# Two weight sums of the mLSTM values built by VectorE instead of accumulating transfers, in a Strassen-like product on one Trainium2 core

## The chip, the cores and the metric

The kernel runs on one core of a Trainium2 chip. The metric is the device time of one execution in microseconds; of several executions the median is taken. TensorE (PE) multiplies, VectorE (DVE) and ScalarE (ACT) do elementwise work, GpSimd (POOL) some more of it; transfers are issued from the queues of SyncE (SP), ScalarE and POOL.

## What is computed

One decoder block with two branches, on x of 512 x 1024 in float32: RMSNorm, one wide input projection, an mLSTM branch (4 heads of 256, chunked in the reference), a sparse attention branch (8 heads of 64), gates, two branch projections, one output projection, residual and RMSNorm. Cut to what the change touches:

```python
hN = _rmsnorm(x, norm_g[l])
p = _split_in(hN @ w_in[l])          # w_in: 1024 x 8992
mh = _mlstm(mq, mk, p["m_v"].reshape(B, T, M_HEADS, M_HEAD_DIM), ...)
```

The change lies in the values `m_v`: a product of h (512 tokens x 1024) with the 1024 x 1024 columns of `w_in` that begin at 2048.

## The kernel before

Every float32 operand of a large product is split into a high part (rounded to TensorE's float32r) and a low remainder, and a product is made of three passes: high x high, high x low, low x high. The split of a weight tile is one ScalarE copy (`wh`) and one VectorE subtraction (`wl`); `weights` (L156) loads a raw tile `wr` and splits it, `halves_of` (L1173) splits a tile that lies in SBUF. Each of `wr`, `wh` and `wl` has three buffers. h lies transposed in SBUF, split into `hTh` and `hTl`.

The order of the work comes from a stream of jobs (L176): each job has a load and a generator of matmuls, and the loads of the next two jobs are written before a job's matmuls begin. A scheduler then orders the instructions of each engine ahead of the run, by their place in the program and by what its own timing takes for ready; on the chip each engine follows its order.

The values are made by seven products of half-sized blocks in place of eight (Strassen's scheme in Winograd's form). h is cut into four quarters of 256 tokens x 512 channels, the weights into quarters W00, W01, W10, W11 of 512 x 512 (`wq[i][j]`: rows i, columns j). A product is 24 matmuls of 128x128 on 128x512 and two jobs, one for each half (`q`) of its 512 channels; `strip_product` (L1202) writes them, two blocks of 128 tokens (`l`) after one another in two PSUM banks. In their order the products use

1. h quarter 0 with W00 (into bank X; copied into Y),
2. h quarter 1 with W10 (onto X, then stored as values),
3. a sum of h (S1) with W00 + W01 (`first_sum`, bank V),
4. a sum of h (S2) with W00 + W01 + W11 (`second_sum`, onto Y),
5. a sum of h (S3) with W11 (`last_quarter`, onto V, then combined by VectorE and stored),
6. a sum of h (S4) with W01 + W11 (`third_sum`, onto Y, then combined and stored),
7. h quarter 3 with W00 + W01 + W11 + W10 (`fourth_sum`, onto Y, then stored).

The weight sums lie in `E`, two tiles of 128 x 4 x 512. They are built by transfers alone: `onto` (L1098) either loads a 512 KB half from memory through SP's queue or adds it in flight to what lies there, through POOL's queue. E[0] begins as W00 + W01, is split for the third product, and is then loaded anew as W01 + W11 for the sixth. E[1] begins as W00 + W01 + W11, is split for the fourth product, and then gets W10 added for the seventh. That makes six plain loads and ten accumulating ones. E, and the tiles for the sums of h, lie in memory that attention used before, so none of this can begin before attention's last instruction.

The sums of h (`sum_of_h`, L1118) are VectorE's: the first (two joined quarters, a difference, a split) stands ahead of the first product, the second in the first product's second job, the third in the second product's first job, a difference that the fourth needs (`a11 - a21`, number 0) in its second job, the split of the fourth in the fourth product's first job.

Around the products: two gate projections (48 matmuls) run just before, and the projections of q and k for the first head (`convs(0)`, L1287) just behind, all 128-column jobs of the stream (L214 to L218).

Of the kernel before, what the change touches and what calls it, by code (L numbers as in the profile page):

```python
# [11 lines left out]
F32 = mybir.dt.float32  # L12
# [66 lines left out]
def build(  # L79
# [1015 lines left out]
    def piece_of(src, q):  # L1095
        return src[:, 2 * q : 2 * q + 2]

    def onto(e, q, i, j, add=True):  # L1098
        if add:
            nc.gpsimd.dma_start(piece_of(E[e], q), piece_of(wq[i][j], q), accum_op=OP.add)  # L1100
        else:
            nc.sync.dma_start(piece_of(E[e], q), piece_of(wq[i][j], q))

    for q in range(2):
        onto(0, q, 0, 0, False)
        onto(0, q, 0, 1)
    for q in range(2):
        onto(1, q, 0, 0, False)
        onto(1, q, 0, 1)
        onto(1, q, 1, 1)  # L1110
    gates_ahead(2, sg0)

    a21, a22, a11, a12 = whole = [raws(i, (4, 256), f"r{i}") for i in range(4)]
# [59 lines left out]
    def halves_of(raw):  # L1173
        hi = wp.tile([128, 2, 512], F32R, name="wh", tag="wh", bufs=3)
        lo = wp.tile([128, 2, 512], F32R, name="wl", tag="wl", bufs=3)
        split(raw, hi, lo)
        return hi, lo

    def first_sum(q):
        w = halves_of(piece_of(E[0], q))  # L1180
        if q:
            E[0] = st.tile([128, 4, 512], F32, name="E", tag="E0")
            for i in range(2):
                onto(0, i, 0, 1, False)
                onto(0, i, 1, 1)
        return w

    def second_sum(q):
        w = halves_of(piece_of(E[1], q))
        onto(1, q, 1, 0)  # L1190
        return w

    def last_quarter(q):
        return from_w(1, 1)(q)

    def third_sum(q):
        return halves_of(piece_of(E[0], q))

    def fourth_sum(q):
        return halves_of(piece_of(E[1], q))  # L1200

    def strip_product(lhs, load, bank, first, post, pre=((), ())):  # L1202
        def gen(q):
            def run(w):
                for n in pre[q]:
                    sum_of_h(n)
                for l in range(2):
                    ps = bank(l)
                    for j in range(2):
                        a, b = lhs(2 * q + j, l)  # L1210
                        c, d = w[0][:, j], w[1][:, j]
                        begin = first and q + j == 0
                        pe.matmul(ps, a, c, start=begin, stop=False, skip_group_check=not first)  # L1213
                        yield
                        pe.matmul(ps, a, d, start=False, stop=False, skip_group_check=not first)  # L1215
                        yield
                        pe.matmul(ps, b, c, start=False, stop=q + j == 2, skip_group_check=not first)  # L1217
                        if l + j < 2:
                            yield
                    if q == 1:  # L1220
                        post(l)

            return run

        for q in range(2):
            stream.add(lambda q=q: load(q), gen(q))
# [10 lines left out]
    def negated(ps, t):  # L1237
        dve.scalar_tensor_tensor(t, ps, -1.0, t, OP.mult, OP.subtract)
        return t

    sum_of_h(1)
    strip_product(of_h(0), from_w(0, 0), X, True, after1, ((), (2,)))
    strip_product(of_h(1), from_w(1, 0), X, False, lambda l: store_values(l, 0, X(l)), ((3,), (0,)))
    strip_product(of_sum(1), first_sum, V, True, after5)
    strip_product(of_sum(2), second_sum, Y, False, after6, ((4,), ()))
    strip_product(
        of_sum(3), last_quarter, V, False, lambda l: store_values(l, 1, negated(V(l), kept["p12"][:, l]))
    )
    strip_product(
        of_sum(4), third_sum, Y, False, lambda l: store_values(2 + l, 1, negated(Y(l), kept["p22"][:, l]))  # L1250
    )
    strip_product(of_h(3), fourth_sum, Y, False, lambda l: store_values(2 + l, 0, Y(l)))

# [489 lines left out]
```

## Time and profile before

| | |
|---|---|
| median of three runs | 634.84 us (634.75 to 635.98) |
| the profiled execution | 636.86 us, span 634.8 us |
| granted TensorE clock, mean | 0.988 |
| PE, DVE, ACT, POOL busy | 613.4, 450.8, 326.2, 89.7 us |
| loads into E: plain (SP), accumulating (POOL) | 6 and 10, of 512 KB |

The profile is of one execution. Busy time of an engine is the time in which it had an instruction in flight; matmuls overlap, so their pace is read from start to start. An idle time is put down to the instruction or transfer that ended it. Most lines of the listing appear as L94, since a helper there issues all instructions of ScalarE, VectorE and POOL; they are told apart by their tiles. `pp`, `ps`, `pt` are the PSUM banks: in this stage `ps` is X, `pt` is V and `pp` is Y. L1213, L1215 and L1217 are the three passes of `strip_product`.

### The profile page before, as it was taken

To read this page: it belongs to the slowest core of one execution; us is meant where nothing else is said; L and a number is where in the kernel's file an instruction comes from. 1 tells how busy PE (TensorE), PEld (TensorE's weight loads), DVE (VectorE), ACT (ScalarE), POOL (GpSimd) and SP (SyncE) were. 2 spreads that over 40 slices of the span, in tenths; PEclk is the share of its full clock that TensorE was granted. 3 is DMA by queue.
4 is the path that set the end of the run, shared out by engine and by line. 5 is a ranking of instruction groups with operands and counts; after the bars stand their busy time and mean duration, and the time that the engine had idled before them with its cause. 6 is when DMAs were issued, how large, how long until landed. Compare 5 with 4: busy or idle time off the path is not lost.

```text
span 634.8 us, 8493 instructions
## 1 busy us (share of the span) xinstructions
PE 613.4 (97%) x3033; PEld 510.0 (80%) x3033; DVE 450.8 (71%) x860; ACT 326.2 (51%) x621; POOL 89.7 (14%) x169
## 2 busy tenths in 40 slices
PE   8999999999999999999499999999999999999995
PEld 6988888888788888787378888888888888888884
DVE  5876776876766956678376788787687665358885
ACT  5775556556546557444356445545445222334554
POOL 6320012212322213212300000000000100000013
PEclk9999999999999999999699999999999999999998
DMA  9546522221222122249954313223222266333313
GB/s 294 153 115 182 136 81 66 68 65 36 68 67 67 42 62 64 62 165 254 203 116 130 100 35 99 73 68 93 67 93 74 66 215 177 108 101 132 132 34 133
DMA packets 92410, 68.14 MB, mean 107 GB/s; under 512 B 3104, under 2 KB 80068, under 8 KB 92368
## 3 DMA queue, kind: packets, MB, share of 16 engines
q1 hardware_dynamic: 89070, 61.30, 33.7%
q0 software_dynamic: 2720, 5.24, 4.6%
q10 hardware_dynamic: 578, 1.05, 0.4%
q8 instruction: 24, 0.39, 0.3%
q14 instruction: 18, 0.15, 0.1%
HBM read 64.44 MB, written 2.10 MB: 105 GB/s over the span
## 4 chain that ended last, share of the span: by engine, by line
PE 47%; DMA 4%; DVE 3%; ACT 1%; POOL 1%; issue 1%; ACTq 0%; POOLq 0%; SPq 0%; DVEq 0%
PE pp L216 12%; PE pp L214 12%; PE pp L218 12%; DMA E<-w_in 4%; DVE wl L94 1%; PE ps L174 1%; DVE s L94 1%; PE pp L1215 1%; PE pp L1213 1%; PE ps L173 1%; PE ps L172 1%; PE pp L1217 1%; PE pt L1360 1%; PE pt L1362 1%; PE pt L1361 1%
## 5 line engine op out<-in xcount | busy, mean ns | idle before, releaser
L214 PE MATMUL pp<-hTh,wh 128*128 128x512 f32 (+1 forms) x488 | 191.5, 392 | 0.0
L216 PE MATMUL pp<-hTl,wh 128*128 128x512 f32 (+1 forms) x488 | 190.9, 391 | 0.0
L218 PE MATMUL pp<-hTh,wl 128*128 128x512 f32 (+1 forms) x488 | 190.6, 391 | 0.0
L94 DVE TENSOR_TENSOR wl<-wr,wh 128x1024 fp32r<-128x1024 f32 x84 | 103.4, 1233 | 38.0 <-ACT wh L94 36.7
L94 ACT ACTIVATE wh<-wr 128x1024 fp32r<-128x1024 f32 x84 | 88.8, 1058 | 72.3 <-PE pp L216 47.4
L218 PEld LDWEIGHTS pp<-hTh,wl 128*128 128x128 f32 x488 | 91.9, 188 | 16.4
L214 PEld LDWEIGHTS pp<-hTh,wh 128*128 128x128 f32 x488 | 91.9, 188 | 16.1
L216 PEld LDWEIGHTS pp<-hTl,wh 128*128 128x128 f32 x488 | 92.0, 189 | 15.6
L94 POOL TENSOR_SCALAR P<-P,st,gates 128x128 f32<-128x128 f32 (+1 forms) x64 | 45.2, 720 | 186.7 <-DVE st L94 136.2
L94 ACT ACTIVATE P<-P,st 128x128 f32<-128x128 f32 (+3 forms) x64 | 35.8, 559 | 38.1 <-DVE st L94 37.6
L94 DVE CUSTOM_DVE_ANT_0 P<-ps,cst 128x128 f32<-128x128 f32 (+3 forms) x64 | 30.4, 486 | 23.0 <-PE ps L939 21.8
L94 ACT ACTIVATE pth<-pt 128x512 fp32r<-128x512 f32 (+1 forms) x64 | 26.8, 435 | 29.0 <-PE pt L955 22.3
L94 DVE TENSOR_TENSOR ptl<-pt,pth 128x512 fp32r<-128x512 f32 (+1 forms) x64 | 30.1, 483 | 14.4 <-ACT pth L94 14.2
L94 DVE SCALAR_TENSOR_TENSOR u<-pp,prm,u 128x511 f32<-128x511 f32 (+2 forms) x48 | 35.7, 744 | 0.7
L94 ACT ACTIVATE th<-u 128x512 f32<-128x512 f32 x16 | 10.1, 631 | 41.5 <-DVE u L94 41.5
L94 POOL TENSOR_TENSOR rlr<-va,mhalf 128x4 f32<-128x4 f32 x4 | 5.1, 1287 | 184.6 <-DVE va L94 184.6
L955 PE MATMUL pt<-cst,P 128*128 128x128 f32 x160 | 28.8, 277 | 1.8 <-POOL P L94 1.0
L955 PEld LDWEIGHTS pt<-cst,P 128*128 128x128 f32 x160 | 20.1, 141 | 11.6 <-DVE ptl L94 4.8
L214 PE MATMUL pp<-yah,wh 128*128 128x512 f32 x64 | 24.9, 389 | 0.0
L216 PE MATMUL pp<-yal,wh 128*128 128x512 f32 x64 | 24.9, 389 | 0.0
L218 PE MATMUL pp<-yah,wl 128*128 128x512 f32 x64 | 24.9, 389 | 0.0
L968 PE MATMUL po<-ptl,vsw 128*128 128x512 f32 (+1 forms) x64 | 21.2, 332 | 0.0
(378 smaller groups left out, 1135.1 us busy)
## 6 DMA issues: line engine op xcount, KB each, us to landing
wr<-w_in SPq DMA_DIRECT2D x66, 512.0 KB, 3.9
E<-w_in POOLq DMA_DIRECT2D x10, 512.0 KB, 8.7
wr<-w_out SPq DMA_DIRECT2D x8, 512.0 KB, 3.9
wr<-w_branch_a SPq DMA_DIRECT2D x8, 512.0 KB, 4.4
E<-w_in SPq DMA_DIRECT2D x6, 512.0 KB, 5.6
wr<-w_branch_b SPq DMA_DIRECT2D x4, 512.0 KB, 3.5
T<-w_out SPq DMA_DIRECT2D x4, 512.0 KB, 5.0
s<-x SPq DMA_DIRECT2D x8, 256.0 KB, 4.0
```

Of the source, the lines that this page charges most:

```text
L94: ins = fn(*args, **kw)
L172: pe.matmul(ps, a, c, start=start and i == 0, stop=False)
L173: pe.matmul(ps, a, d, start=False, stop=False)
L174: pe.matmul(ps, b, c, start=False, stop=stop and i == n - 1)
L214: pe.matmul(ps, a, c, start=k == 0, stop=False)
L216: pe.matmul(ps, a, d, start=False, stop=False)
L218: pe.matmul(ps, b, c, start=False, stop=k == nk - 1)
L955: pe.transpose(pt[:, (qb - kb) * 128 : (qb - kb) * 128 + 128], P[:, POFF[qb] + kb * 128 : POFF[qb] + kb * 128 + 128], ident,)
L968: pe.matmul(po[:, kb * 128 :], vl, tl[:, :n], start=False, stop=False)
L1213: pe.matmul(ps, a, c, start=begin, stop=False, skip_group_check=not first)
L1215: pe.matmul(ps, a, d, start=False, stop=False, skip_group_check=not first)
L1217: pe.matmul(ps, b, c, start=False, stop=q + j == 2, skip_group_check=not first)
```

## The change

The weight sums of the third and of the sixth product are no longer accumulated in flight. E[0] is loaded as W01 alone, and E[1] later, after the split of the third product's sum, as W01 alone. The raw tile of W00, which the first product loads anyway, is added to E[0] by VectorE right behind its split (`first_quarter`), and the raw tile of W11, which the fifth product loads, to E[1] (`last_quarter`). So E[0] is W00 + W01 for the third product. Then W11 is added to it in flight for the fourth, and W10 for the seventh: one tile serves three products in turn. E[1] becomes W01 + W11 for the sixth. There are four plain loads, four accumulating ones and four additions on VectorE.

The sums of h are moved: the first into the first product's first job, the second and third into the two jobs of the second product, a11 - a21 into the third product's first job, the fourth where it was. They come one per job.

The sixth product is written block by block: its first job only holds its weights back, and its second writes all twelve matmuls of the first block and then all twelve of the second.

```diff
     for q in range(2):
-        onto(0, q, 0, 0, False)
-        onto(0, q, 0, 1)
-    for q in range(2):
-        onto(1, q, 0, 0, False)
-        onto(1, q, 0, 1)
-        onto(1, q, 1, 1)
+        onto(0, q, 0, 1, False)
     gates_ahead(2, sg0)
...
+    def plain(i, j, q, e):
+        raw = wp.tile([128, 2, 512], F32, name="wr", tag="wr", bufs=3)
+        nc.sync.dma_start(raw, piece_of(wq[i][j], q))
+        w = halves_of(raw)
+        dve.tensor_tensor(piece_of(E[e], q), piece_of(E[e], q), raw, OP.add)
+        return w
+
+    def first_quarter(q):
+        return plain(0, 0, q, 0)
+
     def first_sum(q):
         w = halves_of(piece_of(E[0], q))
-        if q:
-            E[0] = st.tile([128, 4, 512], F32, name="E", tag="E0")
-            for i in range(2):
-                onto(0, i, 0, 1, False)
-                onto(0, i, 1, 1)
+        onto(0, q, 1, 1)
+        onto(1, q, 0, 1, False)
         return w
 
     def second_sum(q):
-        w = halves_of(piece_of(E[1], q))
-        onto(1, q, 1, 0)
+        w = halves_of(piece_of(E[0], q))
+        onto(0, q, 1, 0)
         return w
 
     def last_quarter(q):
-        return from_w(1, 1)(q)
+        return plain(1, 1, q, 1)
 
     def third_sum(q):
+        return halves_of(piece_of(E[1], q))
+
+    def fourth_sum(q):
         return halves_of(piece_of(E[0], q))
...
-    def strip_product(lhs, load, bank, first, post, pre=((), ())):
+    def strip_product(lhs, load, bank, first, post, pre=((), ()), whole=False):
+        held = []
+
         def gen(q):
             def run(w):
                 for n in pre[q]:
                     sum_of_h(n)
+                held.append((q, w))
+                if whole and q == 0:
+                    return
                 for l in range(2):
                     ps = bank(l)
-                    for j in range(2):
-                        a, b = lhs(2 * q + j, l)
-                        c, d = w[0][:, j], w[1][:, j]
-                        begin = first and q + j == 0
+                    todo = [(k, v[0][:, k % 2], v[1][:, k % 2]) for i, v in held for k in (2 * i, 2 * i + 1)]
+                    for k, c, d in todo:
+                        a, b = lhs(k, l)
+                        begin = first and k == 0
...
                     if q == 1:
                         post(l)
+                held.clear()
...
-    sum_of_h(1)
-    strip_product(of_h(0), from_w(0, 0), X, True, after1, ((), (2,)))
-    strip_product(of_h(1), from_w(1, 0), X, False, lambda l: store_values(l, 0, X(l)), ((3,), (0,)))
-    strip_product(of_sum(1), first_sum, V, True, after5)
+    strip_product(of_h(0), first_quarter, X, True, after1, ((1,), ()))
+    strip_product(of_h(1), from_w(1, 0), X, False, lambda l: store_values(l, 0, X(l)), ((2,), (3,)))
+    strip_product(of_sum(1), first_sum, V, True, after5, ((0,), ()))
     strip_product(of_sum(2), second_sum, Y, False, after6, ((4,), ()))
...
     strip_product(
-        of_sum(4), third_sum, Y, False, lambda l: store_values(2 + l, 1, negated(Y(l), kept["p22"][:, l]))
+        of_sum(4), third_sum, Y, False, lambda l: store_values(2 + l, 1, negated(Y(l), kept["p22"][:, l])),
+        whole=True,
     )
```

More of the change, by code (lines that the diff above doesn't have):

```diff
@@ L1177, in halves_of @@
         return hi, lo
+    def plain(i, j, q, e):
[6 more added lines that the diff above has]
+        return plain(0, 0, q, 0)
     def first_sum(q):
         w = halves_of(piece_of(E[0], q))
-        if q:
-            E[0] = st.tile([128, 4, 512], F32, name="E", tag="E0")
-            for i in range(2):
-                onto(0, i, 0, 1, False)
-                onto(0, i, 1, 1)
+        onto(0, q, 1, 1)
+        onto(1, q, 0, 1, False)
         return w
     def second_sum(q):
-        w = halves_of(piece_of(E[1], q))
-        onto(1, q, 1, 0)
+        w = halves_of(piece_of(E[0], q))
+        onto(0, q, 1, 0)
         return w
     def last_quarter(q):
-        return from_w(1, 1)(q)
+        return plain(1, 1, q, 1)
     def third_sum(q):
+        return halves_of(piece_of(E[1], q))
+    def fourth_sum(q):
         return halves_of(piece_of(E[0], q))
-    def fourth_sum(q):
-        return halves_of(piece_of(E[1], q))
-    def strip_product(lhs, load, bank, first, post, pre=((), ())):
+    def strip_product(lhs, load, bank, first, post, pre=((), ()), whole=False):
+        held = []
         def gen(q):
@@ L1216, in run @@
                         yield
-                        pe.matmul(ps, b, c, start=False, stop=q + j == 2, skip_group_check=not first)
-                        if l + j < 2:
+                        pe.matmul(ps, b, c, start=False, stop=k == 3, skip_group_check=not first)
+                        if l == 0 or k != todo[-1][0]:
                             yield
```

## The prediction

> **What bounds the kernel now.** The page first: the share of each engine, and PE and its granted clock in forty slices (15.9 us each).
>
> ```profile
> PE 613.4 (97%) x3033; PEld 510.0 (80%) x3033; DVE 450.8 (71%) x860; ACT 326.2 (51%) x621; POOL 89.7 (14%) x169
> PE   8999999999999999999499999999999999999995
> PEclk9999999999999999999699999999999999999998
> ```
>
> TensorE bounds everything except one slice, the twentieth (302 to 317 us), where it is busy for 4 tenths and its clock falls. Second view, TensorE's waits over the whole span: after the start there is one that matters, and it ends on ScalarE's split of a weight sum.
>
> ```profile
> PE pp L1213 <- ACT wh L94: 8.0, 1, 8.0
> ```
>
> Third, the chain that ended last (start, us, what) says who is late.
>
> ```profile
> 278.85 3.81 DMA E<-w_in
> ...
> 298.76 9.19 DMA E<-w_in
> 308.03 1.06 ACT wh L94
> 309.12 1.23 DVE wl L94
> 310.40 0.79 PE pp L1215
> ```
>
> The fourth product's weights are a load and two accumulating transfers in series behind other accumulating transfers: 29 us from the opening of the pool at 278.85 to the split at 308.03. Fourth view, TensorE's timeline around the seven products, with the window from the first product to the first matmul behind the seventh and the two windows behind it (us, then busy us of PE, PEld, DVE, ACT, POOL, then clock, DMA share, GB/s).
>
> ```profile
> 284.64 0.39 PE L1213 MATMUL ps<-wh,hTh 128*128 128x512 f32 x1
> 289.85 0.39 PE L1217 MATMUL ps<-wh,hTl 128*128 128x512 f32 x1
> 300.73 0.39 PE L1217 MATMUL pt<-wh,S 128*128 128x512 f32 x1
> 309.14 0.79 PE L1213 MATMUL pp<-wh,S 128*128 128x512 f32 x1 [8.02 <-ACT wh L94]
> ```
> ```profile
> 316.05 0.40 PE L1217 MATMUL pp<-wh,S 128*128 128x512 f32 x1
> 329.24 0.40 PE L1325 MATMUL ps<-ghl,sel 128*128 128x512 f32 x1
> 329.84 0.47 PE L1213 MATMUL pp<-wh,hTh 128*128 128x512 f32 x1 [0.20 <-DVE p L94]
> 335.38 0.39 PE L214 MATMUL pp<-hTh,wh 128*128 128x512 f32 x1
> ```
> ```profile
> 284.64:335.38 50.74, 42.05 (x170) 33.57 (x169) 32.98 (x34) 25.64 (x35) 11.02 (x10) 0.90 0.88 196
> 335.38:607.00 271.62, 271.59 (x1293) 226.83 (x1292) 197.83 (x336) 122.48 (x198) 5.15 (x4) 1.00 0.36 103
> ```
>
> From 284.64 to 300.73 lie 71 steps: 0.2266 us from start to start. The seven products are 7 x 24 = 168 matmuls, 38.07 us at that pace; the one other matmul in between (L1325) adds 0.23. They took 50.74, so **12.44 us are lost here**: 8.41 - 0.23 = 8.18 waiting ahead of the fourth product; 3.74 in the 14 steps from 309.14 to 316.05 (6.91 against 3.17), which hold the wait for the low half, split until 309.12 + 1.23 = 310.35 by the chain, and a half clock; 0.52 in the small rest, of which 0.37 lies between 329.24 and 329.84, where the seventh product waits for VectorE to read the sixth's bank. Behind 335.38 PE is busy for 271.59 of 271.62 us: what is won here reaches the end whole, and nothing behind it can give more.
>
> **The change, part by part.** A product is two jobs of 12 matmuls (2.72 us); at full pace the jobs begin at 284.64 + 2.72 n: third product 295.52, fourth 300.96, fifth 306.40, sixth 311.84, seventh 317.28, end 322.72.
>
> *Removed:* six of ten accumulating transfers and two of six plain loads. The fourth product's sum is no longer built beside the third's; it is the third's sum with one quarter added in place.
>
> *Added:* four VectorE additions of 128x1024. The nearest rows are the additions of the same shape, and the split beside them:
>
> ```profile
> L94 DVE TENSOR_TENSOR r<-r,r 128x1024 f32<-128x1024 f32 x2 | 2.4, 1216 | 0.0
> L94 DVE TENSOR_TENSOR wl<-E,wh 128x1024 fp32r<-128x1024 f32 x8 | 9.8, 1226 | 15.8 <-ACT wh L94 15.8
> L94 ACT ACTIVATE wh<-E 128x1024 fp32r<-128x1024 f32 x8 | 8.5, 1059 | 17.9 <-DMA E<-w_in 14.4 <-PE pt L1217 2.8 <-ACT yah L94 0.7
> 278.85:284.64 5.79, 5.79 (x28) 4.78 (x26) 5.77 (x6) 2.57 (x4) 1.33 (x2) 1.00 0.87 296
> 284.64:300.96 16.32, 16.32 (x73) 13.33 (x71) 13.86 (x13) 8.66 (x12) 4.95 (x5) 1.00 1.10 256
> 316.05:323.58 7.53, 7.53 (x35) 6.19 (x33) 3.65 (x4) 3.71 (x5) 0.00 (x0) 1.00 1.12 239
> ```
>
> Two of them (2 x 1.22) fall before the fourth product. VectorE is busy for 5.77 + 13.86 = 19.63 of the 22.11 us there; with them it is 22.06: full. What makes room is that the third sum of h (three instructions) and a11 - a21 (one) run in that stretch but are wanted only at 306.40 and 311.84: 4 x 1.22 = 4.9 us that can slide. But much of the idle time they could slide into (15.8 us ahead of the splits of E, second row) was the stall itself, and goes with it. Over the whole stage, 278.85 to 322.72, VectorE had 5.77 + 32.98 us of work up to 335.38; four additions make it 43.6 of 43.9. Of that, these belong to jobs behind the seventh product:
>
> ```profile
> 330.58 1.23 DVE L94 TENSOR_TENSOR wl<-wr,wh 128x1024 fp32r<-128x1024 f32 x1 [0.29 <-ACT wh L94]
> 334.01 1.23 DVE L94 TENSOR_TENSOR wl<-wr,wh 128x1024 fp32r<-128x1024 f32 x1 [0.21 <-ACT wh L94]
> ```
>
> So it has about 41 us of work in 43.9: it fits, with little room, where each split must be in time for its job. If an addition were not covered it would cost 1.22, all four 4.9. I take **0.5** for a split of the fifth or sixth product that comes late behind them.
>
> *Kept but moved:* the path that now sets the fourth product. Its rows, from the timelines of ScalarE, POOL and SP's queue:
>
> ```profile
> 287.56 1.07 ACT L94 ACTIVATE wh<-wr 128x1024 fp32r<-128x1024 f32 x1 [1.40 <-PE ps L1217]
> 291.50 1.06 ACT L94 ACTIVATE wh<-E 128x1024 fp32r<-128x1024 f32 x1 [0.55 <-DMA E<-w_in]
> 283.31 3.89 POOL L1100 DMA_DIRECT2D E<-w_in  x3 [5.50 <-DMA E<-w_in]
> 310.65 3.68 POOL L1100 DMA_DIRECT2D E<-w_in  x3 [4.93 <-DVE wl L94]
> 297.48 0.89 SPq L1102 DMA_DIRECT2D E<-w_in  x2
> 282.39 8.31 SPq L159 DMA_DIRECT2D wr<-w_in  x3
> 276.08 0.37 SPq L159 DMA_DIRECT2D wr<-w_in  x1
> ```
>
> The split tiles have three buffers, so the third product's first split waits for the end of the first product's second job (289.85 + 0.39 = 290.24), as the row at 287.56 waits for the job before it. ScalarE 290.3 to 291.35, VectorE to 292.6, POOL 0.3 later (in the trace 309.12 + 1.23 = 310.35, then 310.65). How long one accumulating transfer takes, from issue to landing, for three issues: the one at 310.65, with no plain load beside it; that at 298.76, with the two plain loads of 297.48 beside it; the worst pair (287 to 289), with others ahead of it.
>
> ```profile
> E<-w_in POOLq DMA_DIRECT2D x1, 512.0 KB, 5.7
> ```
> ```profile
> E<-w_in POOLq DMA_DIRECT2D x1, 512.0 KB, 9.2
> ```
> ```profile
> E<-w_in POOLq DMA_DIRECT2D x2, 512.0 KB, 13.2
> ```
>
> Alone: lands 292.9 + 5.7 = 298.6, ScalarE done at 299.75, VectorE at 301.0, against 300.96 and, for the second matmul, 301.19. So the margin is 1.2 us on the high part and 0.2 on the low part. The second half: its buffer comes free at 292.96 + 0.16, so split done 295.4, landing 301.4, high part 302.5, low part 303.7, against 303.68 and 303.91: the same. One VectorE instruction in the way (1.22) costs 1.0 us, once, since what delays the first half also gives the second its time. I take **1.2** for what is left of the wait, nearest to the 5.7 row because nothing else accumulates then and the plain loads (the second quarter-sum's included) are ready to go from 278.85 on; the ends are 0 and 4.5 (below). A wait of 1.2 us does not cost the clock: it fell at 305.74 (0.87 of the us is 0.74 at full and 0.26 at half), 4.8 us into the wait, and the matmul at 316.05 took 0.40 again.
>
> ```profile
> 305.00:306.00 1.00, 0.00 (x0) 0.00 (x0) 0.00 (x0) 0.00 (x0) 0.72 (x1) 0.87 1.13 209
> ```
>
> The Trainium skill, "TensorE: Matmul & The Clock Gate", Part 1, says that the clock is halved after an idle window of about 3.4 us and comes back after a busy one; the trace's half clock (305.7 to 316.0, about 10.2 us) is three such windows, so by that rule an unlucky 3.4 us wait could already halve it. The Trainium skill, "SBUF — State Buffer", SBUF: two separate sides, speaks against the change: VectorE holding the port pair it shares with GpSimd keeps GpSimd from writing the descriptors of its transfers. Here three issues in a row took 3.89 us from 283.31, with VectorE full, and 3.68 from 310.65: 0.07 us more each; by the rule, one VectorE instruction ahead of the critical issue, my sum would be 1.2 us worse.
>
> *First quarter's raw buffer.* It is now held until the addition, which needs the plain load of E (278.85 + 3.81 = 282.66): so the raw load for the second product's second job, issued at 276.08 before, goes out near 284.6 in SP's queue, with the fifth product's behind it. Here are the loads of E issued from 278 to 280:
>
> ```profile
> E<-w_in SPq DMA_DIRECT2D x3, 512.0 KB, 4.8
> ```
>
> Even at 4.8 us to land and a split of 2.3 it is done by 291.7, wanted at 292.80: nothing, cover 1.1 us.
>
> *Sums of h later:* the first is wanted at 295.52 and is four instructions that can run from 278.85: nothing.
>
> *Sixth product block by block:* both its halves are wanted within 1.36 us. The second waits for a buffer until 309.1 + 0.2, is split at 311.6, wanted at 313.20: nothing. The seventh's second half gets its buffer after matmul 18 (316.1), split 318.4, wanted 320.0: nothing. The first bank is free 2.7 us ahead, so the 0.37 goes; the second bank has 1.36 us for VectorE's 0.68 behind a possible 1.23: I keep **0.3**.
>
> Sum: 12.44 - 1.2 - 0.5 - 0.3 = **10.4 us** gained. The profiled execution took 636.86 us over a span of 634.8; it stands 2.0 us above the median of the runs (634.84), and the 2.1 us around the span are no part of the change. So the span goes to 624.4, its time to 626.5, and the median to **624.4**.
>
> **The rivals.** (a) *The wait stays, smaller: transfers collide.* The accumulating transfer meets plain loads as the 9.2 us one did, with VectorE one instruction late: 294.1 + 9.2 = 303.3, high part 304.45, a wait of 3.5 and 1.0 more for the low part: 4.5 us. 634.84 - (12.44 - 4.5 - 0.8) = 627.7. For it: the last of the three raw loads from 282.39 to 290.70 and the second quarter-sum's could fall into 293 to 299. Against: the six transfers that filled the engines then are gone. (b) *VectorE becomes the bound.* Its order is fixed ahead; if the first addition stands second in it, VectorE stands still until 282.66, and all behind it, the third product's split among it, is up to 3.8 us late: landing 302.4, high part 303.5, low part 304.7: 3.6 us lost, and with 0.8 for the rest 626.8; with all four additions uncovered (4.9) 628.1. For: it is full to 0.05 us. Against: 4.9 us can slide. (c) *Slower:* one buffer now carries split, addition in place, split, addition, split in strict series, so a late landing cannot be overtaken. If the critical transfer has three ahead of it and takes 17 us (worst row 13.2), the high part is done at 311.0: 10.1 us, plus 3.74 for the clock and the low part, against 12.44: 1.4 us and the 0.8 slower, 637.0. It decides from a landing of 14.8 us up; against it, only two accumulations are issued before it is needed.
>
> **How the numbers follow.** Forecast 0.60, (a) 0.14, (b) 0.18, (c) with its neighbourhood (landings from 13 us up, from a small gain to a loss) 0.08. The forecast's own bounds are 0 to 3.2 us left over: 622.4 to 625.6. The range takes in (a) and (b) and a little below the best case, for a changed order of instructions: 621.8 to 628.6. What a measurement of this kernel can tell from no change is about 0.2%, 1.3 us. Faster 0.92, no change 0.03, slower 0.05, all from these cases.
>
> **What would show it.** Right: the 8.0 us wait gone from TensorE's waits, 168 matmuls in about 40.1 us, no half clock between 295 and 320, four POOL issues of E instead of ten, four VectorE rows E<-E,wr near 1.22 us. Wrong in the chain: an L1213 wait on ACT wh with E's landing above 6 us (a), or with VectorE's split later than 293.8 (b). Wrong in the last step: a wait on DVE p over 0.5 us. A span above 629 would mean that the wait was not removed but moved.

## The result: 10.1 us less

| | before | after |
|---|---|---|
| median of six runs each, us | 635.38 (634.75 to 636.56) | 625.3 (624.54 to 627.18) |
| the profiled execution, us | 636.86, span 634.8 | 627.18, span 624.9 |
| the seven products, first matmul to the first one behind them, us | 50.74 | 41.08 |

The ratio is 0.9844, with a 95% interval of 0.9825 to 0.9862: 10.1 us gained, where 10.4 were forecast (624.4). Of the 0.9 us by which the time itself missed, 0.5 are before's median, 635.38 here and 634.84 when the forecast was made. Three single executions among the runs below took 1015 to 1229 us and are left out of every ratio. The profiled execution of the changed kernel is the slowest of its six; the spans of the others lie between 622.7 and 624.6 us. Further down a second and a third profile of the same kernel tell what belongs to that one execution.

The page of the changed kernel, its first part and two lines of its second, answers the rows shown of before:

```profile
PE 610.6 (98%) x3033; PEld 507.8 (81%) x3033; DVE 454.4 (73%) x864; ACT 326.8 (52%) x621; POOL 82.6 (13%) x163
PE   7999999999999999999899999999999999999995
PEclk9999999999999999999999999999999999999998
```

The slice with 4 tenths and the clock at 6 tenths is gone; one slice, again the twentieth, has 8 tenths at full clock. VectorE has four instructions more (864 for 860), POOL six issues fewer.

TensorE's waits inside the stage, and the windows view of the stage (us, then busy us of PE, PEld, DVE, ACT, POOL, then clock, DMA share, GB/s):

```profile
PE pp L1220 <- ACT wh L94: 0.8, 1, 0.8
PE pp L1222 <- DVE wl L94: 0.8, 1, 0.8
...
PE ps L1220 <- ACT pp L94: 0.4, 1, 0.4
```
```profile
284.70:325.78 41.08, 39.09 (x170) 31.30 (x169) 35.49 (x37) 25.54 (x32) 5.01 (x4) 1.00 0.61 146
```

One wait of 8.0 us has become three that make 2.0, and the granted clock of the stage is 1.00 in place of 0.90. (L1220, L1222 and L1224 are what L1213, L1215 and L1217 were.) At the pace of 0.2267 us the 168 matmuls take 38.09, so 2.99 us are lost here now, against 12.44 in before. TensorE's timeline shows where; each row is the first matmul behind a gap, its own wait in brackets:

```profile
290.69 0.50 PE L1220 MATMUL ps<-wh,hTh 128*128 128x512 f32 x1 [0.39 <-ACT pp L94]
...
302.71 0.51 PE L1220 MATMUL pp<-wh,S 128*128 128x512 f32 x1 [0.84 <-ACT wh L94]
...
303.97 0.50 PE L1222 MATMUL pp<-wl,S 128*128 128x512 f32 x1 [0.76 <-DVE wl L94]
```

Counted from start to start beyond the pace, the second product loses 0.55 and 0.11 (at 290.69 and behind it), the fourth 1.00 at its high part (302.71), 1.03 at its low part (303.97) and 0.10 behind that, all the rest of the stage together 0.2. Four additions and four issues stand in the view of the tile E (duration ns min/median/max, first and last start):

```profile
L94 DVE TENSOR_TENSOR E<-E,wr x4: 1216/1218/1226, 282.6 to 310.9; 128x1024 f32<-128x1024 f32 x4
...
L1100 POOL DMA_DIRECT2D E<-w_in x4: 1194/1197/1421, 295.5 to 306.8; - x4
```

The chain that ended last, through the path to the fourth product (start, us, what):

```profile
278.91 3.68 DMA E<-w_in
282.61 1.24 DVE E L94
283.87 5.14 DMA wr<-w_in
289.09 1.07 ACT wh L94
...
291.33 2.36 DVE r L94 x2
293.68 1.14 DVE wl L94
294.87 0.59 issue
295.46 6.05 DMA E<-w_in
301.60 1.07 ACT wh L94
302.69 1.24 DVE wl L94
```

It is read from the top: the addition waits for the plain load of E, the raw tile's buffer for the addition, ScalarE for the raw tile, VectorE works two instructions of the sums of h, then splits the third product's sum; only then may the accumulating transfer be issued, and it takes 6.05 us to land. The links stood in the prediction with shorter times, but for `r L94 x2`, which it had only as one instruction that could come in the way. The timelines of VectorE and ScalarE around the split:

```profile
291.33 1.22 DVE L94 SCALAR_TENSOR_TENSOR r<-r,r 128x1024 f32<-128x1024 f32 x1
292.46 1.22 DVE L94 TENSOR_TENSOR r<-hTh,hTl 128x1024 f32<-128x1024 f32 x1
293.60 1.22 DVE L94 TENSOR_TENSOR wl<-E,wh 128x1024 fp32r<-128x1024 f32 x1
```
```profile
289.09 1.06 ACT L94 ACTIVATE wh<-wr 128x1024 fp32r<-128x1024 f32 x1 [1.51 <-DMA wr<-w_in]
290.06 1.06 ACT L94 ACTIVATE pp<-ps 128x512 f32<-128x512 f32 x2
291.05 1.05 ACT L94 ACTIVATE wh<-E 128x1024 fp32r<-128x1024 f32 x1
```

The high part is ready at 291.05 + 1.05 = 292.10, but the joined quarter at 292.46, which the third sum of h needs and TensorE wants only for the fifth product, goes first: 1.14 us. ScalarE stood idle for 1.51 us ahead of 289.09, waiting for the raw tile of the second product's second half; the copies of bank X into Y stand behind it in its order, and the second product, which writes on in X, waits for them.

### The profile page after: what moved, and what is told of

The parts are those of the page before. It is cut to its first block, busy times and chain, and to the rows that moved or that the text cites. A ratio compares the mean times of both kernels' runs of the same rounds, so it can differ in the third digit from the quotient of the medians.

```text
span 624.9 us, 8475 instructions
## 1 busy us (share of the span) xinstructions
PE 610.6 (98%) x3033; PEld 507.8 (81%) x3033; DVE 454.4 (73%) x864; ACT 326.8 (52%) x621; POOL 82.6 (13%) x163
## 3 DMA queue, kind: packets, MB, share of 16 engines
q10 hardware_dynamic: 578, 1.05, 0.5%
## 4 chain that ended last, share of the span: by engine, by line
PE 48%; DVE 3%; DMA 2%; ACT 1%; POOL 1%; issue 1%; ACTq 0%; POOLq 0%; SPq 0%; DVEq 0%
PE pp L216 12%; PE pp L214 12%; PE pp L218 12%; DMA E<-w_in 2%; DVE wl L94 1%; PE pp L1222 1%; PE ps L174 1%; DVE s L94 1%; PE pp L1224 1%; PE pp L1220 1%; DMA wr<-w_in 1%; PE ps L173 1%; PE ps L172 1%; PE pt L1368 1%; PE pt L1370 1%
## 5 line engine op out<-in xcount | busy, mean ns | idle before, releaser
L94 DVE TENSOR_TENSOR wl<-wr,wh 128x1024 fp32r<-128x1024 f32 x84 | 103.5, 1234 | 36.6 <-ACT wh L94 35.3
L94 ACT ACTIVATE wh<-wr 128x1024 fp32r<-128x1024 f32 x84 | 88.7, 1057 | 70.1 <-PE pp L216 48.4
L94 POOL TENSOR_SCALAR P<-P,st,gates 128x128 f32<-128x128 f32 (+1 forms) x64 | 45.5, 726 | 186.1 <-DVE st L94 135.9
L94 ACT ACTIVATE P<-P,st 128x128 f32<-128x128 f32 (+3 forms) x64 | 35.8, 559 | 37.9 <-DVE st L94 37.5
L94 DVE CUSTOM_DVE_ANT_0 P<-ps,cst 128x128 f32<-128x128 f32 (+3 forms) x64 | 30.5, 486 | 22.9 <-PE ps L939 21.8
L94 ACT ACTIVATE pth<-pt 128x512 fp32r<-128x512 f32 (+1 forms) x64 | 26.9, 435 | 29.0 <-PE pt L955 22.3
L94 DVE TENSOR_TENSOR ptl<-pt,pth 128x512 fp32r<-128x512 f32 (+1 forms) x64 | 30.2, 484 | 14.5 <-ACT pth L94 14.2
L94 DVE SCALAR_TENSOR_TENSOR u<-pp,prm,u 128x511 f32<-128x511 f32 (+2 forms) x48 | 35.8, 745 | 0.8
L94 ACT ACTIVATE th<-u 128x512 f32<-128x512 f32 x16 | 10.1, 632 | 39.3 <-DVE u L94 39.3
L94 POOL TENSOR_TENSOR rlr<-va,mhalf 128x4 f32<-128x4 f32 x4 | 5.1, 1286 | 181.4 <-DVE va L94 122.3
```

The source lines that it names most:

```text
L94: ins = fn(*args, **kw)
```

## The experiments

The theory: the 8 us wait and its half clock came from late weight sums, and VectorE's additions remove them; the moved sums of h and the block-by-block product matter little; what is left is the one accumulating transfer between third and fourth product. The rivals: the gain comes from the moved work; or the wait that remains is VectorE's order and not the transfer; or the second accumulation could go to VectorE as well. The stage is measured in each run as above (first matmul of the first product to the first behind the seventh), the time as the median of its runs beside runs of before on the same chip. In some runs one matmul of another job (0.23 us, L1325 in before) falls into the stage; their stages are marked "with one matmul more". The diffs are against the changed kernel, except the one that says otherwise.

### The parts one by one

The weight sums alone: the sums of h at their old places, the sixth product in two jobs.

```diff
-    strip_product(of_h(0), first_quarter, X, True, after1, ((1,), ()))
-    strip_product(of_h(1), from_w(1, 0), X, False, lambda l: store_values(l, 0, X(l)), ((2,), (3,)))
-    strip_product(of_sum(1), first_sum, V, True, after5, ((0,), ()))
+    sum_of_h(1)
+    strip_product(of_h(0), first_quarter, X, True, after1, ((), (2,)))
+    strip_product(of_h(1), from_w(1, 0), X, False, lambda l: store_values(l, 0, X(l)), ((3,), (0,)))
+    strip_product(of_sum(1), first_sum, V, True, after5)
...
-        whole=True,
```

> Only the weight sums are changed (four additions on VectorE, four accumulating transfers); the sums of h stand where they stood before, and the sixth product is written in two jobs. Theory (the 8.2 us wait was the queue of accumulating transfers, and taking six of them away is the whole gain): the wait of 8.2 us is gone, the stage from the first matmul of the first product to the first behind the seventh takes 40.5 to 42 us (41.1 in the changed kernel, 50.7 before), with 0.3 to 0.5 us more ahead of the seventh product; the median lies at 625 to 626.5. Rival (the move of the sums of h is needed, since VectorE is full up to the fourth product): the third product's first split on VectorE comes 2 us or more later than 293.6 and the stage takes 43.5 us or more, median above 627.5.

Measured: 625.97 us, ratio 0.9848 (0.9833 to 0.9862), stage 40.99 with one matmul more. Two of TensorE's waits in it:

```profile
PE ps L1220 <- ACT pp L94: 0.7, 1, 0.7
PE pp L1220 <- DVE p L94: 0.4, 1, 0.4
```

The weight sums alone bring the whole gain. The wait on `DVE p` at the seventh product (0.60 from start to start) is the one that before had.

The reverse, before with the moved sums of h and the block-by-block product, and the weight sums by transfers as they were (the diff cut to its core):

```diff
     for q in range(2):
-        onto(0, q, 0, 1, False)
+        onto(0, q, 0, 0, False)
+        onto(0, q, 0, 1)
+    for q in range(2):
+        onto(1, q, 0, 0, False)
+        onto(1, q, 0, 1)
+        onto(1, q, 1, 1)
...
-        return plain(1, 1, q, 1)
+        return from_w(1, 1)(q)
...
-    strip_product(of_h(0), first_quarter, X, True, after1, ((1,), ()))
+    strip_product(of_h(0), from_w(0, 0), X, True, after1, ((1,), ()))
```

> The kernel before with the sums of h moved and the sixth product block by block; the weight sums stay with the six loads and ten accumulating transfers. Theory: the wait ahead of the fourth product stays, 7.5 to 8.5 us, with a half clock behind it; stage 50 to 51 us, median 634.3 to 635.5. Rival (the moved sums of h free the split and so the transfers earlier): wait below 6 us, stage below 48 us.

Measured: 634.96 us, ratio 0.9995 (0.9985 to 1.0005), stage 49.04 in the profiled execution. TensorE's wait in it, and the stage's row in the windows view:

```profile
PE pp L1228 <- ACT wh L94: 8.0, 1, 8.0
```
```profile
285.44:334.48 49.04, 40.62 (x170) 32.63 (x168) 31.08 (x33) 24.54 (x32) 10.81 (x9) 0.90 0.89 195
```

The wait is untouched and the time is that of before. The stage is 1.7 us shorter in the profile, for L1325's 0.23 and the 0.37 at the seventh product are gone and less of the half clock falls on work. Two one-us windows give its ends, by the mean clock in each:

```profile
304.00:305.00 1.00, 0.00 (x0) 0.00 (x0) 0.00 (x0) 0.00 (x0) 0.14 (x1) 0.62 1.12 299
...
314.00:315.00 1.00, 1.00 (x5) 0.82 (x4) 1.00 (x1) 1.00 (x2) 0.98 (x1) 0.76 0.96 147
```

It lasted from 304.24 to 314.48, again 10.24 us, and so 4.6 us past the end of the wait (309.88) where before had 6.8. That is how the execution fell; over ten of them nothing of it shows in the time.

Two more leave out one of the smaller parts. Only the sums of h back at their old places:

```diff
-    strip_product(of_h(0), first_quarter, X, True, after1, ((1,), ()))
...
+    sum_of_h(1)
+    strip_product(of_h(0), first_quarter, X, True, after1, ((), (2,)))
...
```

> The changed kernel with the sums of h put back to their old places; VectorE's weight sums and the block by block sixth product stay. Theory: the move of the sums is worth less than 0.7 us, since the order on VectorE is made by what is ready and not by the place in the program alone; stage 40.5 to 41.8 us, median 624.7 to 626. Rival: VectorE does the sums of h first and the additions late, stage 43.5 us or more, median above 627.5.

And only the block-by-block order taken away:

```diff
-        whole=True,
```

> The changed kernel with the sixth product in two jobs again; weight sums and the places of the sums of h as changed. Theory: the block by block order is worth the wait ahead of the seventh product alone: 0.3 to 0.5 us more there than in the changed kernel, stage 41.3 to 41.7 us, median 625.3 to 626. Rival (it costs, since the sixth product wants both its halves within 1.36 us): stage shorter than 40.9 us.

Measured: with the old places a ratio of 0.9844 (0.9824 to 0.9865) and a stage of 40.24; without the block-by-block order 626.43 us, 0.9862 (0.9842 to 0.9883), and 41.00 (both with one matmul more). Both intervals hold the ratio of the whole change, so the times tell neither part from nothing. In the timelines, the first loses less at the fourth product (0.56 and 0.21 in place of 1.00 and 1.14) and 0.95 at the second: there the raw load that waits for the first addition goes out 0.02 us after the stage's first matmul, and in the changed kernel 0.83 ahead of it. The weight sums alone show the same (0.03 after it, 1.02 us lost at the second product). So in these single profiles the moved sums of h gain at one product about what they cost at the other. The run without the block-by-block order brings back the wait at the seventh product, 0.37 from start to start, and among TensorE's waits:

```profile
PE pp L1220 <- DVE p L94: 0.2, 1, 0.2
```

So the block-by-block order does what the prediction said, and it is worth 0.4 us in the trace.

### Without the accumulation between third and fourth product

W11 is not added for the fourth and the seventh product; all else stays.

```diff
     def first_sum(q):
         w = halves_of(piece_of(E[0], q))
-        onto(0, q, 1, 1)
         onto(1, q, 0, 1, False)
```

> The changed kernel without the accumulating transfer of W11 between the third and the fourth product: the fourth and the seventh product leave W11 out, all instructions of the three computing engines stay. Theory (what is left ahead of the fourth product, 2.2 us, hangs on this transfer and on the split it waits for): no wait of TensorE at the fourth product; stage 38.6 to 39.2 us against 41.1, median 622.7 to 623.6. Rival (VectorE is the bound there, the transfer would be hidden): at least 1.5 us stay ahead of the fourth product, stage above 40.3 us.

Measured: 622.93 us, ratio 0.981 (0.9793 to 0.9826), stage 38.19, and TensorE has no wait in it. The stage's row in the windows view:

```profile
283.61:321.80 38.19, 38.19 (x170) 31.49 (x168) 35.16 (x37) 25.62 (x32) 2.62 (x2) 1.00 0.50 128
```

168 x 0.2267 are 38.09, so all other products together lose 0.1 us. What is left of the wait in the changed kernel is the path through this one transfer; nothing else in the stage costs anything that shows, not the splits of the fifth and sixth products behind the additions and not the second bank of the seventh.

The same transfer taken out of before (W11 is missing in its fourth and seventh products; the diff is against before):

```diff
         onto(1, q, 0, 1)
-        onto(1, q, 1, 1)
```

> The kernel before without the two accumulating transfers that add W11 to the second weight sum: the fourth and the seventh product leave W11 out. Theory (the wait was the series of transfers: the fourth product's last one was issued only at 298.76 and took 9.2 us): with the transfer before it landing at 298.5, the high part is ready at 299.6 and the wait is below 1 us for the first half, below 1.5 us for the second, with no half clock; stage 39 to 41 us. Rival (the wait has another cause, ScalarE's or VectorE's order): 4 us or more remain, with a half clock.

Measured in one execution: 630.56 us, span 628.7, stage 45.68 (with one matmul more) and not 39 to 41. The fourth product's wait is gone, but among TensorE's waits there is one of the sixth product:

```profile
PE pp L1212 <- ACT wh L94: 2.1, 1, 2.1
```

Its weight sum is E[0] loaded anew, and the chain shows its landing as late:

```profile
303.43 1.02 POOL E L1100
...
304.88 10.75 DMA E<-w_in
...
315.74 1.06 ACT wh L94
```

10.75 us for an accumulating transfer with three more issued beside it (POOL at 303.43, four in a row in the timeline). In before the 8 us wait at the fourth product gave that transfer its time. So the transfers were late twice, and with the first late one alone taken away 5.0 us were gained (635.54 to 630.56, one execution): both had to come off the path, and the change does that, since its sixth product's sum is VectorE's.

### The order on VectorE, and on SP's queue

VectorE's join, its difference a11 - a21 and the additions to E[1] keep their place in the program, behind the splits:

```diff
...
-            whole_h(a12, 1)
+            tc.keep_in_program_order(whole_h(a12, 1))
...
-            dve.tensor_tensor(a21, a11, a21, OP.subtract)
+            tc.keep_in_program_order(dve.tensor_tensor(a21, a11, a21, OP.subtract))
...
-        dve.tensor_tensor(piece_of(E[e], q), piece_of(E[e], q), raw, OP.add)
+        add = dve.tensor_tensor(piece_of(E[e], q), piece_of(E[e], q), raw, OP.add)
+        if e:
+            tc.keep_in_program_order(add)
```

> The changed kernel with four of VectorE's instructions (joining a12, a11 - a21, and the two additions to E[1]) kept behind the splits that are written ahead of them, so that the third product's first split is not behind one of them. Theory: that split on VectorE begins at 292.3 to 292.6 in place of 293.60, the accumulating transfer goes out near 294.0 in place of 295.46, and what is lost at the fourth product falls from 2.2 to 1.0 to 1.2 us; stage 39.9 to 40.1 us, median about 624.2. Rival (VectorE is full, so what moves back there makes something else late; or the landing sets it whatever the issue): stage 40.8 us or more.

Measured: 624.98 us, ratio 0.9838 (0.9824 to 0.9853), stage 40.04. The split, the issue and the next split, from the timelines of VectorE, POOL and ScalarE:

```profile
290.76 1.23 DVE L94 TENSOR_TENSOR wl<-E,wh 128x1024 fp32r<-128x1024 f32 x1
```
```profile
292.63 1.42 POOL L1100 DMA_DIRECT2D E<-w_in  x1 [15.98 <-DVE wl L94]
```
```profile
298.70 1.06 ACT L94 ACTIVATE wh<-E 128x1024 fp32r<-128x1024 f32 x1 [3.54 <-DMA E<-w_in]
```

Counted from each stage's first matmul, the split begins at 7.28 us (8.90 in the changed kernel's first profile, 8.03 in its second) and the issue at 9.15 (10.76, 9.88). The high part is now in time; TensorE's waits are for the low parts of both halves:

```profile
PE pp L1224 <- DVE wl L94: 1.1, 2, 0.8
```

At the fourth product 1.14 and 0.61 are lost, in place of 2.0: the second half's low part has become late, because a11 - a21 now stands ahead of it on VectorE. Of the 0.7 us by which the issue came earlier than in the second profile, 0.2 are left in the stage, and the intervals of the times do not tell that from nothing.

The loads of E[1] keep their place too, behind the raw load, in SP's queue:

```diff
-            nc.sync.dma_start(piece_of(E[e], q), piece_of(wq[i][j], q))
+            load = nc.sync.dma_start(piece_of(E[e], q), piece_of(wq[i][j], q))
+            if e:
+                tc.keep_in_program_order(load)
```

> The changed kernel with the two loads of E[1] kept in SP's queue behind the raw load of the second product's second job. Theory (that raw load, let go late by the addition, landed at 289.0 beside the loads of E[1]; ScalarE's split stood waiting for it, with the copies of the first product's banks behind it, and TensorE waited 0.4 us for such a copy): the raw tile lands by 287.8, the wait for ScalarE's copy is gone, the second product begins without a gap; stage 40.4 to 40.6 us in place of 41.1. Rival (the copy is late for another reason): the gap of 0.55 us at the second product stays.

Measured: 625.69 us, ratio 0.9845 (0.9828 to 0.9862), stage 40.27, and no wait at the second product. That would speak for the edit, if the changed kernel itself always had that wait. It has not. Profiled again, beside the next experiment and beside the last one:

> The changed kernel as it is, on the chip of the next run and against the same runs of the kernel before. Every theory: 10 us faster than before (9.4 to 10.6), stage 41.1 us.

> The changed kernel as it is, beside the version with W11 added by VectorE. Every theory: stage 40.2 to 41.1 us, about 10 us faster than the kernel before.

Measured: 625.61 us (0.9861, 0.9846 to 0.9876), stage 40.24; and 625.66 us (0.985, 0.9831 to 0.9868), stage 40.22. ScalarE's wait for the raw tile in the second profile:

```profile
286.69 1.06 ACT L94 ACTIVATE wh<-wr 128x1024 fp32r<-128x1024 f32 x1 [0.41 <-DMA wr<-w_in]
```

0.41 us where the first had 1.51, and no wait of TensorE at the second product in either. So the 0.66 us lost there belong to that execution of the changed kernel and not to all of them. What the edit of the queue is worth stays open.

Both edits together (the diffs are those two):

> Both edits together: VectorE's four instructions kept behind the splits, and the loads of E[1] kept behind the raw load. Theory (the two losses stand in series on the path to the fourth product: the late raw tile shifts ScalarE's split of the third product's sum by 0.75 us, VectorE's order by 1.14 more): stage 38.7 to 39.4 us, 1.7 to 2.4 us less than the changed kernel beside it, median 622.9 to 623.6. Rival (they do not add up, since the margin is the transfer's landing): stage 39.9 us or more.

Measured: ratio 0.9844 (0.983 to 0.9857), 0.9861 (0.9846 to 0.9876) for the changed kernel beside it, stage 40.07. I had expected 38.7 to 39.4; the losses are 1.13 and 0.65 at the two low parts of the fourth product, as with the first edit alone; among TensorE's waits:

```profile
PE pp L1226 <- DVE wl L94: 1.2, 2, 0.8
```

The step that failed in that expectation was to add up two gains of which one was not there in most executions, and to hold the path for short enough once VectorE was free. It isn't: split, issue, 6.1 us of landing, high part, low part.

### W11 by VectorE as well

The raw tile of W11 is loaded two products earlier and added to E[0] by VectorE; it stays in its buffer for the fifth product. Two accumulating transfers (W10) remain.

```diff
     def first_sum(q):
+        raw = raw11[q] = wp.tile([128, 2, 512], F32, name="wr", tag="wr", bufs=3)
+        nc.sync.dma_start(raw, piece_of(wq[1][1], q))
         w = halves_of(piece_of(E[0], q))
-        onto(0, q, 1, 1)
+        dve.tensor_tensor(piece_of(E[0], q), piece_of(E[0], q), raw, OP.add)
...
```

> The changed kernel, and in addition W11 is added for the fourth product by VectorE too: the raw tile of W11, which the fifth product splits anyway, is loaded in the third product's job and added to E[0] behind the split, in place of an accumulating transfer; two accumulating transfers (W10) are left. Theory (the rest of the loss is the round of split, POOL issue and 6.1 us landing; VectorE idles 2.2 us there, which takes the two additions of 2.4): no wait of TensorE at the fourth product, stage 38.2 to 39.4 us, 1.4 to 2.4 us faster than the changed kernel beside it. Rival (VectorE is full over the whole stage, 41 us of 43.9, and two additions more make it the bound): waits on DVE wl at the fourth, fifth or sixth product of 1.5 us or more together, stage 40.2 us or more, no gain.

Measured: 625.52 us, ratio 0.9841 (0.9826 to 0.9856), against 0.985 (0.9831 to 0.9868) for the changed kernel on the same chip; stage 40.24 with one matmul more. The stage's row in the windows view, TensorE's wait in it, and VectorE's timeline ahead of the split that it ends on:

```profile
284.24:324.48 40.24, 38.75 (x171) 31.58 (x170) 38.26 (x40) 25.85 (x32) 2.62 (x2) 1.00 0.48 121
```
```profile
PE pp L1228 <- DVE wl L94: 1.5, 1, 1.5
```
```profile
299.90 1.22 DVE L94 TENSOR_TENSOR S<-r,S 128x1024 fp32r<-128x1024 f32 x1
...
301.63 1.22 DVE L94 TENSOR_TENSOR wl<-E,wh 128x1024 fp32r<-128x1024 f32 x1
```

The transfer is off the path, and the 2 us did not come: VectorE is busy for 38.26 of the 40.24 us, and without a gap from 282.26 to the end of the low half's split for the fourth product, which begins at 301.63. ScalarE had the high part done at 300.56, but the split of the third sum of h, which only the fifth product wants, and a low part of the second product's values (0.68 us) stood ahead on VectorE. So VectorE's work, in this order, is the bound here, and in the changed kernel, with two additions less, it is not. Whether another order would bring some of the 2 us was not tried.

## Why the prediction was right, point by point

**The stall and its size** (12.44 us lost, nothing behind the stage to give more): right. The sums by VectorE alone bring the whole gain, the rest of the change alone none (0.9995), and with the transfer of W11 gone the stage runs at pace.

**The additions, 1.22 us each, covered:** right. 1216 to 1226 ns, and the stage without the accumulation of W11 loses 0.1 us in all, with all four additions in it.

**What is left at the fourth product, 1.2 us:** too small; it measured 2.13 in the first profile and 2.0 in the other two. The path was the right one, link by link, and every link was longer. From the rows of the first profile, whose stage begins 0.06 us later than before's:

| link | predicted | measured |
|---|---|---|
| ScalarE begins the split of the third product's sum | 290.3 | 291.05 |
| VectorE begins it | 291.35 | 293.60 |
| POOL issues | 292.9 | 295.46 |
| ScalarE begins the split of the new sum | 298.6 | 301.60 |
| low part done | 301.0 | 303.91 |

The 3.0 us of the fourth row are 0.75 on ScalarE, 1.5 on VectorE, 0.34 from the split's end to the issue (0.64 for 0.3) and 0.44 in the landing (6.14 to the use, for 5.7), less 0.03 that the split itself was shorter. In the second profile, without the late raw tile, the same sum is 2.13: 0.54, 0.78, 0.33 and 0.51, less 0.03. The prediction had a margin of 1.2 on the high part and, besides, one VectorE instruction in the way; that instruction was there (1.14 at 292.46), and the other links took the rest of the margin. The second part of the error is the low part. It is done 1.25 us after the high part and wanted 0.23 us after it, so once the high part is late at all, 1.0 us comes on top. I had this 1.0 as the price of any delay, and it is, but as an addition to the high part's own lateness (0.87 to 1.00), which I had put near 0.2. That the second half loses nothing more was right in the changed kernel; it became wrong when the order on VectorE was changed for the first half.

**ScalarE, 290.3:** the step took the split to begin when its buffer came free. But the copy of bank X into Y stands ahead of it in ScalarE's order and waits for the same last matmuls; ScalarE's timeline in the second profile shows it.

```profile
289.20 0.58 ACT L94 ACTIVATE pp<-ps 128x512 f32<-128x512 f32 x1 [0.84 <-PE ps L1224]
289.70 1.05 ACT L94 ACTIVATE wh<-E 128x1024 fp32r<-128x1024 f32 x1
```

It begins 6.20 us after the stage's first matmul here and 6.35 in the first profile, for the 5.66 of the prediction.

**First quarter's raw buffer, "nothing, cover 1.1 us":** right in two profiles, wrong in one. The raw load went out at 283.87, a little before the 284.6 of the prediction, and took 5.1 us where 4.8 had been taken; so it landed at 289.0, still before the predicted 289.4, and its own split was in time. But what waits is not only that split but, in ScalarE's order, the copies of the bank behind it. They were the term that was missing: 0.66 us in that execution, nothing in the others.

**The fifth and sixth products' splits, 0.5, and the seventh's second bank, 0.3:** together with all that is left they cost 0.1 to 0.2. The room on VectorE was larger than the prediction's 43.6 of 43.9, of which it had itself taken some off: from 278.91 to the end of the stage it was busy for 41.08 of 46.87 us (windows view of the first profile):

```profile
278.91:325.78 46.87, 44.88 (x196) 36.07 (x195) 41.08 (x41) 27.09 (x34) 5.01 (x4) 1.00 0.63 161
```

So the sum was 12.44 - 1.2 - 0.5 - 0.3. It came out as 12.44 + 0.23 - 2.13 - 0.66 - 0.2 in the first profile (a stage 9.66 shorter; the 0.23 are the one matmul of another job, L1325 in before, which no longer falls into the stage and is no gain of the whole) and as 12.44 + 0.23 - 2.0 - 0.16 in the second (10.5 shorter). A term too small by 0.8 to 0.9 stands against two that were too large by 0.6 to 0.7 together, so the forecast of the time is nearer than its terms were, and that is luck. Between the medians lie 10.1 us in the first comparison, 9.5 and 9.6 in the other two; all three intervals overlap.

**The clock:** "a wait of 1.2 us does not cost the clock" was right; two waits of 0.8 us, 1.26 us apart, left it at full (1.00 in the stage's row). The half clock has the same length with the wait of 8.0 us in before (305.74 to 315.98, by the mean clock in one-us windows) and in the run without VectorE's sums, 10.24 us, and a third of it in the run that the last section shows. That agrees with the windows of 3413 ns, running on their own, of the Trainium skill, "TensorE: Matmul & The Clock Gate", Part 1.

**The rivals.** (a) The transfers did not collide: the critical one took 6.05 us with no other accumulating one ahead of it, against 9.2 and 13.2 in before, and after 291.44 no plain load was issued until 308.82. The prediction's sign for (a), a landing above 6 us, is met by 0.05 all the same; the sign was drawn too near to the forecast. (b) is half of the truth: VectorE's order was 0.8 to 1.5 us late at the one place that counts, far from its 3.6, and its share was not what bound, until two more additions were given to it (W11 by VectorE). (c) had nothing for it here; the run of before without W11 shows its mechanism, a late landing (10.75 us) that nothing hides, in the kernel before with eight of its ten accumulating transfers. **VectorE and GpSimd's port:** the prediction priced one VectorE instruction, 1.2 us, by a rule of the Trainium skill. That section (the Trainium skill, "SBUF — State Buffer", SBUF: two separate sides) says it of VectorE instructions in a two-port mode, and of those with two inputs in SBUF only against a GpSimd operation that reads SBUF. The instructions beside the issues here are additions and subtractions of two tiles, so the prediction took the rule wider than it is stated. The two issues of the path in the changed kernel, with VectorE's instructions back to back beside both, from POOL's timeline:

```profile
295.46 1.42 POOL L1100 DMA_DIRECT2D E<-w_in  x1 [17.59 <-DVE wl L94]
297.40 1.20 POOL L1100 DMA_DIRECT2D E<-w_in  x1 [0.51 <-DVE wl L94]
```

The second took 1.20 us as before's do; what the first has more is told below, and it did not wait for the end of the VectorE instruction beside it. No wait of that kind shows beside these additions and splits.

## What to carry to other kernels

When a stall is removed, look for the next customer of the same queue: here a second landing was late behind the first, and 8 us of waiting had hidden it, so a cure of the first alone gives half. A path in series through several engines should be priced with what stands ahead of each link in its engine's order, and not with the moment at which its operands are ready: copies and fillers of 0.5 to 1.1 us, harmless anywhere else, made a margin of 1.2 us into a loss of 2. Work moved from a queue to an engine stays free only until that engine is full at the place that counts: four additions on VectorE cost nothing, the fifth and sixth gave nothing.

## What the runs showed of the hardware that was not expected

**The first issue.** POOL's first accumulating issue of the stage begins 0.64 us after the end of the split that it waits for and takes 1.42 us; the next one begins 0.3 us after it and takes 1.20 (the rows just above). The same 1.42 stands in the run without W11, and a later issue for comparison in the one with the splits first:

```profile
299.33 1.42 POOL L1100 DMA_DIRECT2D E<-w_in  x1 [22.55 <-DVE wl L94]
```
```profile
301.32 1.19 POOL L1100 DMA_DIRECT2D E<-w_in  x1 [5.56 <-DVE wl L94]
```

It is the first one whatever VectorE does beside it. The idle time alone doesn't make it: 5.56 us ahead of a later issue do nothing. The first issue of before, at 283.31, took 1.42 too, after 5.50 us of idle time, and the one at 310.65 took 1.20. So the 0.2 between the two rows of three, which the prediction weighed as the port's, is this. Why the first one is slower, no run here tells.

**The half clock after less than 3 us of waiting.** In the run of before without W11 TensorE stood still for 2.1 us ahead of 316.85, did one matmul of 0.50, and stood still for 0.76 more. The clock in windows of one us:

```profile
317.00:318.00 1.00, 0.35 (x1) 0.03 (x1) 1.00 (x2) 0.74 (x1) 0.00 (x0) 0.95 1.11 206
...
321.00:322.00 1.00, 1.00 (x6) 0.77 (x5) 1.00 (x2) 0.00 (x0) 0.00 (x0) 0.85 0.00 1
```

It fell at 317.90 and came back at 321.30: 3.40 us. So a single matmul between two waits did not keep it up, and 2.6 us of waiting, all that had passed by 317.90, were enough. The two waits of the changed kernel have the same form (high part, one matmul, low part) and 1.6 us in all; by this one case their margin to a half clock is an estimated 1.0 us at most.

**The landing of an accumulating transfer** with no other accumulating one ahead of it is 6.1 to 6.2 us from issue to use (6.14 in the changed kernel's first profile, 6.21 in its second, 6.07 with the splits first), for the 5.7 that the prediction took from a later issue; 0.22 of the difference would be the longer first issue.

**The landing of the plain raw load** is not a constant of the program: ScalarE waited for the same tile 1.51 us in one execution and 0.41 in another of the same kernel, and the load took 5.1 us in the first and 4.0 in the other. A cover of 1.1 us is no more than that spread.
